# Latent attention on one core: stacked rotary scores, mask on the Vector engine, halves by shuffle, another order

## The chip, the cores and the metric

The kernel runs on one core of a Trainium2 chip. A core has a matrix engine (TensorE, "PE" in the profile, its weight loads "PEld"), a vector engine (VectorE, "DVE"), a scalar engine (ScalarE, "ACT"), GpSimd ("POOL") and a queue engine (SyncE, "SP") that here issues the transfers. The metric is the device time of one execution in microseconds; smaller is better. Before the change it was 2085.28 us, the median of three runs from 2084.88 to 2087.25.

## What is computed

A decoder of two layers over 256 positions of width 2048, all in f32. The first layer mixes positions by a gated spatial product, the second by latent attention; both attend to 256 memory tokens with 4 heads beside that, and both end in a gated feed-forward part of width 5632 with a convolution of width 3. The change lies in the second layer's attention. Cut to what matters:

```python
def apply_rope(x, cos, sin):
    x1, x2 = jnp.split(x, 2, axis=-1)
    return jnp.concatenate([x1 * cos - x2 * sin, x2 * cos + x1 * sin], axis=-1)

# key/value side, once:  kv = rmsnorm(x, g_kv) @ w_kv_a
c_kv = rmsnorm(kv[..., :512], g_kv_lat)              # latent, 512 wide
k_rope = apply_rope(kv[..., 512:], cos, sin)         # one rotary key, 64 wide, for all heads

q = (rmsnorm(q_lat, g_q_lat) @ w_uq).reshape(B, S, 12, 128 + 64)
q_rope = apply_rope(q[..., 128:], cos, sin)
qa = jnp.einsum('bqhn,rhn->bqhr', q[..., :128], w_uk)
s = (qa . c_kv + q_rope . k_rope) * 192 ** -0.5      # per head
s = jnp.where(k_pos <= q_pos, s, -inf)               # causal
p = softmax(s); o = (p . c_kv) . w_uv                # 12 heads of 128
x = x + concatenate([o, memory_attention]) @ w_out
```

## The kernel before

All activations lie transposed, features on the 128 partitions and the 256 positions along the free axis. TensorE's one-pass mode (type fp32r) keeps fewer bits than f32, so the large products split both operands into a high and a low part and sum three one-pass products: high by high, high by low, low by high (`mm_fm`, lines 137 to 143; activations hold both parts side by side, 512 wide). `chunk` loads a piece of weights (tile `raw`, 4 buffers), and ACT and DVE make its parts `whi` and `wlo`. The small products of attention are plain f32.

The second layer's mixer is `layer_b`. It runs, in this order: the latent of keys and values (`chl`), the query latent (`qhl`), the rotary key, the memory queries, a first third of the values, and then a loop over six pairs of heads. For a pair, `queries` gives two heads' 128 wide parts and, in a third block of 128 rows, both heads' rotary parts, 64 rows each. `rotary` rotates that block: a product with a permuted identity (`swap`, L744) exchanges the halves, POOL and DVE multiply with cosines and sines and add. `keys` gives the pair's keys. `scores` sums three products per block of queries in PSUM: the 128 wide part (L824), the causal mask as a bf16 product with an identity (L825), and the rotary part over 64 rows (L826); the first block of 128 queries sees 128 keys, the second 256. DVE takes the maxima (L832), ACT the exponentials with their sums (L835), DVE divides (L840). `turn` transposes the probabilities (L847) and ACT copies them out of PSUM (L849); `attend` multiplies with the values (L856 to L858) and splits the output into `mainhl`, the operand of the output projection `w_out`. `mscores`, `mturn` and `mout` do the same for the memory heads (L479, L503, L514).

The rotary key of all heads is one block of 64 columns of `w_kv_a`. `chunk(twice=True)` writes its two parts twice side by side, so that the product gives the key on both halves of the partitions, 64 rows each, and a head of either half finds it beside its own rows.

The order of work within an engine is set by a scheduler that models the program's time when it is built, starting from the order in which the code issues it. The code's own order is the loop at the end of `layer_b`: step i issues the queries and keys of pair i, the scores of pair i-1 and the turns and attends of pair i-2; the last two steps and what follows hold the four memory heads; then comes the output projection, heads 0 to 11 first and the memory heads last.

## Time and profile before

| | us |
|---|---|
| median of three runs | 2085.28 |
| the profiled execution | 2085.31 |
| its span (first to last instruction) | 2083.5 |
| TensorE busy in it | 2064.8 |
| DVE, ACT, POOL busy | 1341.7, 1063.4, 108.6 |

A line of the profile's groups names the source line, the engine, the operation, the tile written and those read, the shapes, the number of instructions, their busy time and mean length, and behind the second bar the idle time of the engine ahead of them with what ended it. A line of the timeline has the start and the length in microseconds from the span's start, then the same names; equal instructions that follow each other are merged, and an idle time stands in brackets. Records of products overlap on TensorE, so the distance between two starts, not a record's length, is what a product takes.

### The profile page before, as it was taken

How to read it: one execution, taken by the hardware profiler on the slowest of the kernel's cores; microseconds unless marked ns; L12 is line 12 of the kernel's file. 1: busy time of each engine (PE TensorE's matmuls, PEld its weight loads, DVE VectorE, ACT ScalarE, POOL GpSimd, SP SyncE). 2: the span in 40 equal slices, each digit the busy share in tenths (PEclk: the TensorE clock that was granted, in tenths of full speed). 3: DMA queues.
4: the chain of work that ended last, by engine and by line, in shares of the span. 5: the costliest groups of instructions: out<-in, count | busy, mean ns of one | idle time of the engine just before them, and what ended most of it. 6: DMA issues, size and time to landing. Idle time of an engine off the chain costs nothing.

```text
span 2083.5 us, 39410 instructions
## 1 busy us (share of the span) xinstructions
PE 2064.8 (99%) x16368; PEld 1985.9 (95%) x16368; DVE 1341.7 (64%) x1828; ACT 1063.4 (51%) x1434; POOL 108.6 (5%) x137
## 2 busy tenths in 40 slices
PE   8999999999999999999999999999999999999998
PEld 7989999999999999999999989999988999889996
DVE  6656666766646666467688655676664576655765
ACT  7654644555434554345556555455543555535554
POOL 0000012100000000000052111210000000000000
PEclk9999999999999999999999999999999999999999
DMA  8566556666656666566556534566666666666664
GB/s 275 178 205 189 162 181 197 190 199 191 198 193 192 194 193 200 189 196 193 186 189 187 173 107 133 193 192 187 188 198 196 190 195 193 194 194 193 192 189 151
DMA packets 207575, 392.54 MB, mean 188 GB/s; under 512 B 14302, under 2 KB 22820, under 8 KB 207268
## 3 DMA queue, kind: packets, MB, share of 16 engines
q1 hardware_dynamic: 207252, 389.50, 60.6%
q8 instruction: 128, 2.10, 0.4%
q14 instruction: 51, 0.42, 0.1%
q10 hardware_dynamic: 144, 0.52, 0.1%
HBM read 387.88 MB, written 2.10 MB: 187 GB/s over the span
## 4 chain that ended last, share of the span: by engine, by line
PE 98%; ACT 1%; DMA 0%; issue 0%; DVE 0%; SPq 0%; ACTq 0%
PE ps L141 26%; PE ps L140 26%; PE ps L143 26%; PE ps L171 6%; PE ps L173 6%; PE ps L172 6%; PE ps L826 1%; PE ps L824 1%; DMA raw<-in_w_mem_kv 0%; PE ps L514 0%; PE ps L479 0%; PE ps L659 0%; ACT whi L124 0%; ACT junk L396 0%; PE ps L847 0%
## 5 line engine op out<-in xcount | busy, mean ns | idle before, releaser
L120 DVE TENSOR_TENSOR wlo<-raw,whi 128x1024 fp32r<-128x1024 f32 x660 | 808.4, 1242 | 634.2 <-issue 439.3
L119 ACT ACTIVATE whi<-raw 128x1024 fp32r<-128x1024 f32 x660 | 695.3, 1060 | 785.6 <-PE ps L141 598.0
L140 PE MATMUL ps<-xhl,whi 128*128 128x256 f32 x3280 | 756.1, 277 | 0.0
L141 PE MATMUL ps<-xhl,whi 128*128 128x256 f32 x3280 | 754.3, 276 | 0.0
L141 PEld LDWEIGHTS ps<-xhl,whi 128*128 128x128 f32 x3280 | 615.8, 188 | 0.3
L140 PEld LDWEIGHTS ps<-xhl,whi 128*128 128x128 f32 x3280 | 615.6, 188 | 0.3
L143 PE MATMUL ps<-xhl,wlo 128*128 128x256 f32 x3280 | 406.7, 276 | 0.0
L143 PEld LDWEIGHTS ps<-xhl,wlo 128*128 128x128 f32 x3280 | 387.7, 188 | 0.2
L140 PE MATMUL ps<-h,whi 128*128 128x256 f32 x704 | 161.6, 276 | 0.0
L141 PE MATMUL ps<-h,whi 128*128 128x256 f32 x704 | 161.5, 276 | 0.0
L569 DVE SCALAR_TENSOR_TENSOR c<-a,cT,c 128x255 f32<-128x255 f32 (+1 forms) x352 | 146.1, 477 | 0.0
L172 PE MATMUL ps<-wlo,h 128*128 128x512 f32 x352 | 136.8, 389 | 0.0
L173 PE MATMUL ps<-whi,h 128*128 128x512 f32 x352 | 136.6, 389 | 0.0
L171 PE MATMUL ps<-whi,h 128*128 128x512 f32 x352 | 136.3, 389 | 0.0
L141 PEld LDWEIGHTS ps<-h,whi 128*128 128x128 f32 x704 | 132.0, 188 | 0.0
L140 PEld LDWEIGHTS ps<-h,whi 128*128 128x128 f32 x704 | 131.9, 188 | 0.0
L566 ACT ACTIVATE c<-a,cT 128x256 f32<-128x256 f32 x176 | 91.7, 592 | 75.8 <-DVE a L210 75.8
L140 PE MATMUL ps<-mainhl,whi 128*128 128x256 f32 x512 | 117.9, 276 | 0.0
L141 PE MATMUL ps<-mainhl,whi 128*128 128x256 f32 x512 | 117.7, 276 | 0.0
L125 DVE SCALAR_TENSOR_TENSOR wlo<-raw,gT,whi 128x512 fp32r<-128x512 f32 x112 | 84.5, 801 | 31.6 <-ACT whi L124 28.8
L124 ACT ACTIVATE whi<-raw,gT 128x512 fp32r<-128x512 f32 x112 | 74.9, 717 | 42.2 <-PE ps L141 18.3
L141 PEld LDWEIGHTS ps<-mainhl,whi 128*128 128x128 f32 x512 | 96.1, 188 | 0.0
(256 smaller groups left out, 2060.8 us busy)
## 6 DMA issues: line engine op xcount, KB each, us to landing
raw<-in_w_ffn_up SPq DMA_DIRECT2D x352, 512.0 KB, 3.9
raw<-in_w_ffn_down SPq DMA_DIRECT2D x176, 512.0 KB, 4.4
raw<-in_w_out SPq DMA_DIRECT2D x64, 512.0 KB, 4.0
raw<-in_w_in_a SPq DMA_DIRECT2D x56, 512.0 KB, 3.8
raw<-in_w_mem_kv SPq DMA_DIRECT2D x32, 512.0 KB, 5.2
raw<-in_w_in_b SPq DMA_DIRECT2D x16, 512.0 KB, 4.0
raw<-in_w_uq SPq DMA_DIRECT2D x12, 384.0 KB, 3.0
raw<-in_w_kv_a SPq DMA_DIRECT2D x8, 512.0 KB, 3.8
```

What stands on the lines that cost most here:

```text
L119: nc.scalar.activation(hi[:, :n], raw[:, :n], AF.Copy)
L120: nc.vector.tensor_tensor(lo[:, :n], raw[:, :n], hi[:, :n].bitcast(F32), ALU.subtract)
L124: nc.scalar.activation(hi[:, s], raw[:, s], AF.Copy, scale=gains[k])
L125: nc.vector.scalar_tensor_tensor(lo[:, s], raw[:, s], gains[k], hi[:, s].bitcast(F32), ALU.mult, ALU.subtract)
L140: mm(acc, wh, x[:, :S], start=first, stop=False)
L141: mm(acc, wh, x[:, S:], start=False, stop=False)
L143: mm(acc, wl, x[:, :S], start=False, stop=last)
L171: mm(acc, xh, wh, start=first, stop=False)
L172: mm(acc, xh, wl, start=False, stop=False)
L173: mm(acc, xl, wh, start=False, stop=last)
L566: nc.scalar.activation(c[:, i, :], a[:, i, :], AF.Identity, scale=w(2), bias=w(3))
L569: nc.vector.scalar_tensor_tensor(o, a[:, i, : S - 2 + j], w(j), o, ALU.mult, ALU.add)
```

## The change

The rotary key, the rotary query, the mask and the order of the loop change; all else stays.

*Scores.* A rotated query block of a head is split into its high and low parts, and the two are stacked: for the first head of a pair the high part on rows 0 to 63 and the low part on rows 64 to 127, for the second head the other way round. The key is split likewise into `krs[:, 0]`, its high part on both halves of the rows, and `krs[:, 1]`, its low part on both. Two one-pass products of 128 rows then sum all four products of parts. The mask, -1e30 above the diagonal, is an SBUF tile; one DVE instruction adds it to the scores, writes the sum to `p` and takes the maximum, followed by a read of the accumulator. The exponentials read `p` instead of PSUM.

*Halves.* The host lays out the columns of `w_kv_a` and `w_uq` so that the two halves of a rotary part lie 16 rows apart within 32; a DVE shuffle exchanges them, and DVE does the multiplying and adding. Since the columns of a pair are now in the order in which they are used, `chunk` splits a piece of `w_uq` by one instruction on ACT and one on DVE instead of two.

*Rotary key.* The 64 columns' high and low parts are stacked side by side as one block of 128 columns, each multiplied by both parts of the activations; a product with a folded identity (`fold`) then adds the halves and writes the sum to both.

*Order.* The scores, turns and memory heads of a step are issued as below; the value projections 1 and 2 move to steps 2 and 4, and the output projection starts with the memory heads and takes the last two heads in between.

```diff
         if twice:
-            ...
+            both = hi[:, : 2 * n].rearrange("p (k o c) -> p k o c", o=2, c=ncol)
             for k in range(nk):
-                ...
+                r, h = view(raw)[:, k, :], both[:, k, 0, :]
+                nc.scalar.activation(h, r, AF.Copy, scale=gains[k])
+                nc.vector.scalar_tensor_tensor(both[:, k, 1, :], r, gains[k], h.bitcast(F32), ALU.mult, ALU.subtract)
+            return hi[:, : 2 * n].rearrange("p (k c) -> p k c", k=nk)
...
-            def rotate(dst, a):
-                acc = self.psum()
-                mm(acc[:, :S], self.swap, a, start=True, stop=True)
-                m = self.tmp(lb, [P, S], "rm", 2)
-                nc.gpsimd.tensor_tensor(m, a, self.cosT, ALU.mult)
-                tt(dst, acc[:, :S], self.sinT, ALU.mult)
-                nc.gpsimd.tensor_tensor(dst, dst, m, ALU.add)
+            def rotate(a):
+                other = self.tmp(lb, [P, S], "rs", 2)
+                nc.vector.stream_shuffle(other, a, [i ^ 16 for i in range(32)])
+                r = self.tmp(lb, [P, S], "rm", 2)
+                tt(r, a, self.cosT, ALU.mult)
+                tt(other, other, self.sinT, ALU.mult)
+                tt(r, r, other, ALU.add)
+                return r
...
-                h, l = self.chunk(self.rows(wkv, KR, ROPE)(c, 8), 8, ROPE, [gk(c + i) for i in range(8)], twice=True)
-                self.mm_fm([(acc, h[:, i, :], l[:, i, :], x(c + i), c + i == 0, c + i == NB - 1) for i in range(8)])
-            tt(kr, acc, rb, ALU.mult)
+                both = self.chunk(self.rows(wkv, KR, ROPE)(c, 8), 8, ROPE, [gk(c + i) for i in range(8)], twice=True)
+                for i in range(8):
+                    for o in range(2):
+                        mm(acc, both[:, i, :], x(c + i)[:, o * S : (o + 1) * S], start=c + i + o == 0, stop=c + i + o == NB)
+
+            def rotary_key():
+                nc.scalar.activation(kr, acc, AF.Copy)
+                sums = self.psum()
+                mm(sums[:, :S], self.fold, kr, start=True, stop=True)
+                tt(kr, sums[:, :S], rb, ALU.mult)
+                r = rotate(kr)
+                nc.scalar.activation(krs[:, 0, :], r, AF.Copy)
+                tt(krs[:, 1, :], r, krs[:, 0, :].bitcast(F32), ALU.subtract)
...
+                r = rotate(accs[2])
+                qr[pr] = self.tmp(lp, [P, 2, S], "qr", 2, F32R)
+                for j in range(2):
+                    own, far = (slice(o * ROPE, (o + 1) * ROPE) for o in (j, 1 - j))
+                    nc.scalar.activation(qr[pr][own, j, :], r[own, :], AF.Copy)
+                    tt(qr[pr][far, j, :], r[own, :], qr[pr][own, j, :].bitcast(F32), ALU.subtract)
...
                     mm(o, qn[pr][:, j, q], kn[pr][:, j, :n], start=True, stop=False)
-                    mm(o[:, qb * P :], self.identb, self.maskb, start=False, stop=False)
-                    mm(o, qr[pr][rows, q], krT[rows, :n], start=False, stop=True)
+                    for i in range(2):
+                        mm(o, qr[pr][:, j, q], krs[:, i, :n], start=False, stop=i == 1)
...
-                    nc.vector.tensor_reduce(mx[:, qb : qb + 1], sc[:, part[qb]], AX.X, ALU.max)
+                    nc.vector.tensor_tensor_reduce(
+                        p[:, part[qb]], sc[:, part[qb]], self.mask[:, part[qb]], 1.0, -3e38, ALU.add, ALU.max, mx[:, qb : qb + 1]
+                    )
...
-                mm(o[:, :P], v[:, 0, cols], pT[:, :P], start=True, stop=True)
-                mm(o[:, P:S], v[:, 0, cols], pT[:, P:S], start=True, stop=False)
+                mm(o[:, :S], v[:, 0, cols], pT[:, :S], start=True, stop=False)
                 mm(o[:, P:S], v[:, 1, cols], pT[:, S : S + P], start=False, stop=True)
...
+            for i in range(n):
+                queries(i)
+                keys(i)
+                if i >= 2:
+                    turn(2 * i - 4)
+                    turn(2 * i - 3)
+                if i in (2, 4):
+                    values(i // 2)
+                if i >= 1:
+                    scores(2 * i - 2)
+                    scores(2 * i - 1)
+                if i >= 2:
+                    attend(2 * i - 4)
+                    attend(2 * i - 3)
+                if i < MH:
+                    mscores(i)
+                if 1 <= i <= MH:
+                    mturn(i - 1)
+                if 2 <= i <= MH + 1:
+                    mout(i - 2)
+            each = lambda f, *hs: [lambda h=h: f(h) for h in hs]
+            for f in each(scores, 10, 11) + each(turn, 8, 9) + each(attend, 8, 9):
+                f()
+            hooks = {0: each(turn, 10, 11), 2: each(attend, 10, 11)}
+            self.w_out(1, hl, [12, 13, 14, 15] + list(range(12)), hooks)
             ctx.close()
-            self.w_out(1, hl, list(range(NB)))
```

The new line numbers are some ten lower or higher than the old; the same code is named by both where needed. How the built programs stand, at three places. First TensorE at the scores: before, one head (`kn` keys, `qn` the 128 wide queries, `krT` the rotary key, `qr` the rotary query).

```order
L824 MATMUL ps_13944<-kn_13774,qn_13731 128x128
L825 LDWEIGHTS identb
L825 MATMUL ps_13944<-maskb,identb 128x128
L826 MATMUL ps_13944<-krT,qr_13864 128x128
L824 MATMUL ps_13944<-kn_13774,qn_13731 128x256
L825 LDWEIGHTS identb
L825 MATMUL ps_13944<-maskb,identb 128x128
L826 MATMUL ps_13944<-krT,qr_13864 128x256
```

Now the same place for two heads (L826 is now the 128 wide part, L828 the stacked rotary products).

```order
L826 MATMUL ps_14231<-kn_13967,qn_13954 128x128
L828 MATMUL ps_14231<-krs,qr_13962 128x128 x2
L826 MATMUL ps_14231<-kn_13967,qn_13954 128x256
L828 MATMUL ps_14231<-krs,qr_13962 128x256 x2
L826 MATMUL ps_14249<-kn_13967,qn_13954 128x128
L828 MATMUL ps_14249<-krs,qr_13962 128x128 x2
L826 MATMUL ps_14249<-kn_13967,qn_13954 128x256
L828 MATMUL ps_14249<-krs,qr_13962 128x256 x2
```

A head has six products as before; the two masks and the two 64-row products have become four one-pass products.

Second, TensorE at the end of the loop, before: turns (L847) and attends (L856 to L858) of heads 10 and 11 and the last memory heads.

```order
L847 MATMUL ps_14725<-ident,p_14662 128x128 x3
L479 MATMUL ps_14731<-kT_83,qm_12641 128x256 x2
L479 MATMUL ps_14744<-kT_83,qm_12641 128x256 x2
L847 MATMUL ps_14757<-ident,p_14680 128x128 x3
L856 MATMUL ps_14763<-pT_14729,scratch 128x128
L857 MATMUL ps_14763<-pT_14729,scratch 128x128
L858 MATMUL ps_14763<-pT_14729,scratch 128x128
L856 MATMUL ps_14769<-pT_14761,scratch 128x128
L857 MATMUL ps_14769<-pT_14761,scratch 128x128
L858 MATMUL ps_14769<-pT_14761,scratch 128x128
L503 MATMUL ps_14775<-ident,mp_14737 128x128 x4
L503 MATMUL ps_14782<-ident,mp_14750 128x128 x4
```

Now the end of the loop is the scores of head 11, the turns (L850) and attends (L859, L860) of heads 8 and 9, and the first products of the output projection (L130, L131).

```order
L826 MATMUL ps_14685<-kn_14571,qn_14558 128x128
L828 MATMUL ps_14685<-krs,qr_14566 128x128 x2
L826 MATMUL ps_14685<-kn_14571,qn_14558 128x256
L828 MATMUL ps_14685<-krs,qr_14566 128x256 x2
L850 MATMUL ps_14703<-ident,p_14625 128x128 x3
L850 MATMUL ps_14709<-ident,p_14643 128x128 x3
L859 MATMUL ps_14715<-pT_14707,scratch 128x256
L860 MATMUL ps_14715<-pT_14707,scratch 128x128
L859 MATMUL ps_14720<-pT_14713,scratch 128x256
L860 MATMUL ps_14720<-pT_14713,scratch 128x128
L130 MATMUL ps_14727<-mainhl_13597,whi_14730 128x256
L131 MATMUL ps_14727<-mainhl_13597,whi_14730 128x256
```

No memory head is left here, and nothing stands between the last transpose of heads 8 and 9 and their attends.

Third, ACT at the same place, now: `p_14676` and `p_14694` are the probabilities of heads 10 and 11, `pT_14707` and `pT_14713` the turned ones of heads 8 and 9.

```order
L204 ACTIVATE mainhl_13597<-ps_14652 128x256
L838 ACTIVATE p_14643,den_14642<-p_14643,mx_14641 128x128
L838 ACTIVATE p_14643,den_14642<-p_14643,mx_14641 128x256
L204 ACTIVATE mainhl_13597<-ps_14657 128x256
L204 ACTIVATE mainhl_13597<-ps_14662 128x256
L838 ACTIVATE p_14676,den_14675<-p_14676,mx_14674 128x128
L838 ACTIVATE p_14676,den_14675<-p_14676,mx_14674 128x256
L852 ACTIVATE pT_14707<-ps_14703 128x384
L852 ACTIVATE pT_14713<-ps_14709 128x384
L838 ACTIVATE p_14694,den_14693<-p_14694,mx_14692 128x128
L838 ACTIVATE p_14694,den_14693<-p_14694,mx_14692 128x256
```

The exponentials of head 10 stand ahead of the copies of the turned heads 8 and 9, and those of head 11 behind them.

124 lines of the change are left out of this document (45 added, 79 removed).

## The prediction

> **What bounds the kernel now.** I read the page first: the busy shares, then the chain of waits.
>
> ```profile
> span 2083.5 us, 39410 instructions
> PE 2064.8 (99%) x16368; PEld 1985.9 (95%) x16368; DVE 1341.7 (64%) x1828; ACT 1063.4 (51%) x1434; POOL 108.6 (5%) x137
> PE 98%; ACT 1%; DMA 0%; issue 0%; DVE 0%; SPq 0%; ACTq 0%
> ```
>
> TensorE is busy for 99% of the span and is 98% of the chain that ends last. A change of this kernel is therefore worth what it takes from, or adds to, TensorE's stream of products, plus what TensorE waits. Next the table by stretches, cut where the second layer's latent attention begins (key/value side and query latents until 1160, the loop over head pairs until 1265).
>
> ```profile
> 1083.00:1160.00 77.00, 77.00 (x656) 76.14 (x656) 67.65 (x121) 44.51 (x90) 19.78 (x18) 1.00 0.59 181
> 1160.00:1265.00 105.00, 103.39 (x705) 88.66 (x704) 64.64 (x159) 61.42 (x152) 13.25 (x12) 1.00 0.38 113
> ```
>
> Columns: length, busy us of PE, weight loads, DVE, ACT, POOL (instructions), granted clock, DMA share, GB/s. The clock is full in both. The loop is the only stretch of the two in which PE is not wholly busy, and DVE and ACT work there for 64.6 and 61.4 us of 105. Matmul records overlap, so I price products by the distance from one start to the next in the timeline, not by their duration.
>
> **What a product costs.** Timeline rows (start, length, line, tiles, shape, records). A plain f32 product takes two records, a one-pass (fp32r) product one.
>
> ```profile
> 1185.78 1.07 PE L143 MATMUL ps<-chl,wlo 128*128 128x256 f32 x8
> 1186.69 0.38 PE L824 MATMUL ps<-kn,qn 128*128 128x128 f32 x2
> ...
> 1204.49 0.39 PE L858 MATMUL ps<-pT,scratch 128*128 128x128 f32 x2
> ...
> 1204.96 0.28 PE L140 MATMUL ps<-qhl,whi 128*128 128x256 f32 x1
> ...
> 1257.28 1.89 PE L479 MATMUL ps<-kT,qm 128*128 128x256 f32 x8
> 1259.01 0.49 PE L847 MATMUL ps<-ident,p 128*128 128x128 f32 x3
> 1259.34 0.39 PE L856 MATMUL ps<-pT,scratch 128*128 128x128 f32 x2
> ```
>
> One-pass, 256 columns: (1186.69 - 1185.78) / 8 = 0.114 us. Plain f32, 256 columns: (1259.01 - 1257.28) / 8 = 0.216 a record, 0.43 a product. Transposes of 128 columns: 0.33 / 3 = 0.11. Passing between the two kinds is free within 0.02: from L858 at 1204.49 to the third one-pass record at 1204.96 are 0.47, and one f32 product of 128 columns (0.22, below) and two one-pass ones (0.23) make 0.45.
>
> **Term 1, the scores.** Two heads, then the attend that follows:
>
> ```profile
> 1212.65 0.39 PE L824 MATMUL ps<-kn,qn 128*128 128x128 f32 x2
> ...
> 1213.72 0.70 PE L824 MATMUL ps<-kn,qn 128*128 128x256 f32 x2
> 1214.25 0.22 PE L825 MATMUL ps<-maskb,identb 128*128 128x128 bf16 x1
> 1214.40 0.70 PE L826 MATMUL ps<-krT,qr 64*128 64x256 f32 x2
> 1215.03 0.23 PE L825 MATMUL ps<-maskb,identb 128*128 128x128 bf16 x1
> ...
> 1216.92 0.49 PE L856 MATMUL ps<-pT,scratch 128*128 128x128 f32 x2
> 1217.24 0.39 PE L857 MATMUL ps<-pT,scratch 128*128 128x128 f32 x2
> 1217.46 0.39 PE L858 MATMUL ps<-pT,scratch 128*128 128x128 f32 x2
> ```
>
> An f32 product of 128 columns is 1217.46 - 1217.24 = 0.22. The rotary product L826, only 64 rows high, takes 0.63 (1214.40 to 1215.03) where full height takes 0.43: it is 0.1 late at each record, and the product behind it is late too (the first L856 takes 0.32, not 0.22). So a pair of heads costs 1217.24 - 1212.65 - 0.22 = 4.37, six pairs 26.2 us. After the change a head is an f32 product of 128 columns (0.22) and one of 256 (0.43), two one-pass products of 256 columns (0.23) and two of 128. The mask product and the 64-row products are gone. A one-pass product of 128 columns is nowhere in this trace. Below: the transposes' 0.11; above: a plain f32 product of the same width, 0.22. I take 0.113, since every one-pass row is a single record and the 256-column one needs no more than that. A head is then 0.22 + 0.43 + 0.23 + 0.23 = 1.11, twelve 13.3, and 26.2 - 13.3 = **12.9 us saved**; at the upper bound 24 x 0.11 = 2.6 less.
>
> The Trainium skill speaks against this step: "TensorE: Matmul & The Clock Gate", Part 3, says that a weight load overlaps matmuls in flight only where the two use different row groups, and full-height operands all share theirs. By that rule the 48 stacked loads would stand open. The trace differs: the full-height products at 1257.28 follow each other at 0.216 with nothing exposed, and the 64-row ones are the late ones.
>
> **Term 2, the halves' exchange.** Seven exchange products leave TensorE, one fold product comes in:
>
> ```profile
> 1178.07 0.59 PE L744 MATMUL ps<-qn,swap 128*128 128x256 f32 x2
> 1178.31 0.58 PE L171 MATMUL ps<-whi,chl 128*128 128x512 f32 x1
> 1178.73 0.40 PE L172 MATMUL ps<-wlo,chl 128*128 128x512 f32 x1
> 1178.96 0.39 PE L173 MATMUL ps<-whi,chl 128*128 128x512 f32 x1
> ```
>
> The exchange and one 512-column pass take 0.66, such a pass 0.23, so the exchange 0.43. Six fewer: **2.6 us**.
>
> **Term 3, the rotary key.** 48 one-pass products become 32: 16 x 0.114 = **1.8 us**. The 16 small scalings on ACT and DVE that go with them, and the key's rotation, now behind the fold, lie beside TensorE, which never idles in that stretch (77.00 of 77.00); the rotated key is first read by the first scores (1186.69 now), long after the stretch ends at 1160. Without that cover the key's chain would cost about 3 us once.
>
> **Term 4, waits.** Three now, all at the end of the loop:
>
> ```profile
> 1253.60 1.04 PE L503 MATMUL ps<-ident,mp 128*128 128x128 f32 x8
> 1255.13 1.99 PE L514 MATMUL ps<-pT,mv 128*128 128x256 f32 x8 [0.49 <-ACT pT L507]
> ...
> 1259.79 0.39 PE L858 MATMUL ps<-pT,scratch 128*128 128x128 f32 x2
> 1260.79 0.49 PE L856 MATMUL ps<-pT,scratch 128*128 128x128 f32 x2 [0.62 <-ACT pT L849]
> ...
> 1261.57 0.60 PE L503 MATMUL ps<-ident,mp 128*128 128x128 f32 x4
> 1262.66 0.72 PE L503 MATMUL ps<-ident,mp 128*128 128x128 f32 x4 [0.49 <-DVE mp L495]
> ```
>
> Start to start less the work between: 1.53 - 0.87, 1.00 - 0.22, 1.09 - 0.44, together 2.1, some 2.4 with the first record after each wait, which is 0.1 late. In the new order the memory heads are spread over the loop, and heads 10 and 11 are turned and attended inside the output projection, whose 48 products ahead of each (5.4 us) cover their softmax. Those three waits go. What is late next is the attend of heads 8 and 9: TensorE does the scores of 10 and 11, six transposes, and then needs the evicted transposes, and ACT has the exponentials of head 10 queued ahead of that eviction.
>
> ```profile
> L849 ACT ACTIVATE pT<-ps 128x384 f32<-128x384 f32 x12 | 5.8, 485 | 1.8 <-PE ps L847 1.8
> L835 ACT ACTIVATE p<-ps,mx 128x256 f32<-128x256 f32 x12 | 5.6, 468 | 0.0
> L835 ACT ACTIVATION_READ_ACCUMULATOR p<-ps,mx 128x1 f32 x24 | 4.8, 200 | 0.0
> L832 DVE TENSOR_REDUCE mx<-ps 128x1 f32<-128x256 f32 x12 | 5.0, 413 | 0.0
> L832 DVE TENSOR_REDUCE mx<-ps 128x1 f32<-128x128 f32 x12 | 3.5, 290 | 11.9 <-PE ps L826 11.9
> L801 DVE COPY qn<-ps 128x256 f32<-128x256 f32 x6 | 2.5, 424 | 4.0 <-PE ps L143 3.3 <-issue 0.7
> L747 DVE TENSOR_TENSOR qr<-ps,sinT 128x256 f32<-128x256 f32 x6 | 2.5, 422 | 0.4 <-PE ps L744 0.3
> ```
>
> From the end of head 10's scores: the two masked maxima on DVE, 0.7 (as L832 now) to 1.1 (each with an accumulator read of 0.2, as ACT's), their scaling and the hand-overs about 0.5, two exponentials about 1.0, the eviction 0.5: 2.7 to 3.1. TensorE meanwhile has head 11's scores (1.11) and six transposes (0.66), 1.8. It waits 0.9 to 1.3, and up to 1.3 more if DVE still has the splits of three earlier outputs ahead (3 x 0.42). Behind the waiting eviction on ACT stand the second eviction and head 11's exponentials; the second attend has the first one's 0.65 as cover. I take 1.9 here and 0.5 for the first transposes of the loop, where the pipeline starts with less behind it: 2.4, so this term is **zero**, between 2 lost and 2 gained. The value projections, moved with their four weight DMAs behind two later steps, and the memory scores are the same work elsewhere; DMA is at 0.38 in the loop, and the queue gets no more bytes.
>
> **What is added beside TensorE.** Per pair DVE gets a shuffle, three products and sums and two 64-row differences in place of a copy and a product. By L801 and L747 that is four more at 0.42, 1.7 a pair, 10.1 in all. The masked maximum stands for the plain one; with the reads (2 x 0.2 a head) 4.8 more. A shuffle is not in this trace: at least 0.42 like the copy, twice that if both sides are slow. So DVE has 64.6 + 14.9 = 79.5 us in a loop of about 105 - 15.5 = 89.5: close, but not the bound. ACT gains twelve 64-row copies, some 0.4 each, 4.8 us onto 61.4. POOL loses its share. What hides all this is TensorE's own work between a pair's queries and its scores: the next pair's queries and keys alone are 60 passes of 0.114, 6.8 us.
>
> **Sum:** 12.9 + 2.6 + 1.8 + 0 = 17.3. The profiled execution took 2085.31, its span 2083.5, so 1.8 lie around it; the median of the runs is 2085.28, the same. 2083.5 - 17.3 + 1.8 = **2068.0 us**.
>
> **Rivals.**
> *Narrow one-pass products cost what f32 ones do* (0.22): 2.6 less, 2070.6. For it: no row shows them; against it: they are one record.
> *The late 0.1 stays*: if it comes from a product's neighbours and not its height, each of the 48 stacked products keeps 0.1, 4.8 us: 2072.8. Against it: the free passages above. The skill's rule quoted above leads to the same place.
> *DVE runs behind in the densest steps*: if the 30 new instructions (six shuffles, 24 masked maxima) are dearer by 0.5 each, 15 us fill the 10 us that DVE has left and put 5 on the path: 2073. For it: 79.5 of 89.5 leaves little room, and DVE takes its work in order.
> *DVE becomes the bound, slower than before*: in the loop over pairs, the same 30 instructions. The 10 us left and the 17.3 gained are eaten from 27.3 / 30 = 0.9 us each above what I took; at 1.2 above, 36 - 27.3 gives 8.7 us over before, 2094. Against it: nothing of this width on DVE takes over 0.5 in the rows above.
>
> **How the numbers follow.** Forecast 0.6; narrow products 0.18; neighbours 0.05; DVE behind 0.13; DVE the bound 0.04. The forecast alone spans 2065 to 2071; the range takes in the next three up to 2074: 2064.5 to 2074. This kernel's runs tell about 0.2% (4 us) from no change: faster 0.94, same 0.03, slower 0.03.
>
> **What would show it.** Timeline of a score pair: about 2.2 us instead of 4.37, one-pass products at 0.11 apart. No exchange products, no bf16 mask. In the list of waits one wait of one to two us for an evicted transpose behind the scores of heads 10 and 11, and none in the output projection. DVE at about 80 us in the loop. Wrong would be: narrow products at 0.22, or waits for DVE spread over the steps.

## The result and the profile after

The changed kernel takes 2067.79 us, the median of four runs from 2067.30 to 2069.34; the kernel before, in the same series, 2085.09 (four runs, 2084.88 to 2087.25). The ratio is 0.9914, with a 95% interval from 0.9902 to 0.9926. That is 17.3 us less; 2068.0 us was forecast. The profiled execution took 2069.34 us. Its page, after the change: span, busy times, and the chain that ended last by engine.

```profile
span 2067.6 us, 39221 instructions
...
PE 2048.7 (99%) x16292; PEld 1979.6 (96%) x16292; DVE 1346.7 (65%) x1868; ACT 1064.4 (51%) x1420; POOL 93.2 (5%) x122
...
PE 98%; ACT 1%; DMA 0%; SPq 0%; DVE 0%; issue 0%; DVEq 0%; ACTq 0%
```

TensorE still bounds the kernel, and it is busy 16.1 us less. The span is only 15.9 us shorter, since this one execution came 1.7 us later to the second layer (1094.77 against 1093.03 in the rows below), 1.1 of it in one wait of the first layer, far ahead of the changed code (for `memhl`: 1.3 us before, 2.4 after). This wait differs from execution to execution, also where the first layer's code is the same (1.0 to 2.6 us in the runs below that are made from the changed kernel). I therefore compare a stretch that it doesn't touch: from the first product of the second layer (the sum of squares) to the last product of all. Timeline rows, before:

```profile
1093.03 0.59 PE L244 MATMUL ps<-ssum,ones 128*128 128x256 f32 x2
...
2074.15 0.39 PE L173 MATMUL ps<-whi,h 128*128 128x512 f32 x1
```

and after:

```profile
1094.77 0.59 PE L234 MATMUL ps<-ssum,ones 128*128 128x256 f32 x2
...
2058.22 0.39 PE L163 MATMUL ps<-whi,h 128*128 128x512 f32 x1
```

981.12 us have become 963.45: 17.7 us less, and this is the number that the parts below have to make up. I divided the stretch by adding up, group by group, the distances from the start of each matmul record to the start of the next one. So a wait counts for the group in front of it, and a record that is late too. "Key side" is all from the start of the stretch to the first query product, "memory" the memory heads' three kinds of products. What follows the output projection is 722.09 us in every kernel here.

| us | key side | scores | exchange | turns, attends | memory | queries, keys, values | output projection | stretch |
|---|---|---|---|---|---|---|---|---|
| before | 68.62 | 24.99 | 2.40 | 12.84 | 10.16 | 52.87 | 87.16 | 981.12 |
| after | 66.81 | 13.38 | 0 | 12.76 | 7.84 | 53.32 | 87.25 | 963.45 |
| difference | -1.81 | -11.61 | -2.40 | -0.08 | -2.32 | +0.45 | +0.09 | -17.67 |

One thing shifts between the columns. Where an f32 product stands in front of a one-pass one, the distance behind its last record is 0.03 us instead of 0.22 (256 columns) or 0.11 (128), and the rest of its time is counted with the group behind. Timeline after:

```profile
1197.76 1.03 PE L504 MATMUL ps<-pT,mv 128*128 128x256 f32 x4
1198.44 0.47 PE L130 MATMUL ps<-qhl,whi 128*128 128x256 f32 x1
```

Four records of 0.216 make 0.86, and the distance is 0.68. The memory heads, spread over the loop, have five such places after and one before, the exchange of before has one. Counted where it belongs, the exchange is 2.6 less, memory 1.7 less, and queries, keys and values differ by 0.1.

The loop over pairs of heads, as a window of the profile after (the columns are those of the prediction's):

```profile
1160.00:1265.00 105.00, 103.79 (x784) 98.97 (x783) 74.81 (x211) 72.07 (x161) 0.00 (x0) 1.00 0.44 139
```

DVE does 74.8 us where it did 64.6, ACT 72.1 where it did 61.4, and TensorE idles for 1.2 us. (The window now ends inside the output projection, so part of this is the splitting of its weights: up to 1246.90, just ahead of that projection, DVE does 67.9.) The pair of heads that the prediction priced, in the timeline after:

```profile
1206.09 0.39 PE L826 MATMUL ps<-kn,qn 128*128 128x128 f32 x2
1206.23 0.42 PE L828 MATMUL ps<-krs,qr 128*128 128x128 f32 x2
1206.49 0.65 PE L826 MATMUL ps<-kn,qn 128*128 128x256 f32 x2
1206.78 0.59 PE L828 MATMUL ps<-krs,qr 128*128 128x256 f32 x2
...
1208.32 0.60 PE L859 MATMUL ps<-pT,scratch 128*128 128x256 f32 x2
1208.75 0.38 PE L860 MATMUL ps<-pT,scratch 128*128 128x128 f32 x2
```

From 1206.09 to 1208.32 are 2.23 us, where 2.2 were forecast and 4.37 stood before. Taking off the f32 products (2 x 0.65) and the 256-column one-pass products (4 x 0.114) leaves 0.47 for four narrow ones, 0.12 each. The attend behind isn't late (1208.32 to 1208.75: 0.43).

One wait is left in the loop, the forecast one. TensorE and ACT at the end of the loop, in the timelines after:

```profile
1243.72 0.82 PE L850 MATMUL ps<-ident,p 128*128 128x128 f32 x6
1245.74 0.70 PE L859 MATMUL ps<-pT,scratch 128*128 128x256 f32 x2 [1.21 <-ACT pT L852]
1246.28 0.38 PE L860 MATMUL ps<-pT,scratch 128*128 128x128 f32 x2
```

```profile
1244.33 0.40 ACT L838 ACTIVATE p<-p,mx 128x128 f32<-128x128 f32 x1 [1.76 <-DVE mx L836]
...
1245.22 0.85 ACT L852 ACTIVATE pT<-ps 128x384 f32<-128x384 f32 x2
```

The six transposes need 0.66, so they end about 1244.4; ACT has begun the exponentials of head 10 just before and copies the transposes out only behind them. TensorE loses 2.02 - 0.66 = 1.4, and 0.1 more in the late first record behind (0.54 instead of 0.43).

### The profile page after: what moved, and what is told of

It is laid out like the page before. It is cut to its first block, busy times and chain, and to the rows that moved or that the text cites. A ratio compares the mean times of both kernels' runs of the same rounds, so it can differ in the third digit from the quotient of the medians.

```text
span 2067.6 us, 39221 instructions
## 1 busy us (share of the span) xinstructions
PE 2048.7 (99%) x16292; PEld 1979.6 (96%) x16292; DVE 1346.7 (65%) x1868; ACT 1064.4 (51%) x1420; POOL 93.2 (5%) x122
## 4 chain that ended last, share of the span: by engine, by line
PE 98%; ACT 1%; DMA 0%; SPq 0%; DVE 0%; issue 0%; DVEq 0%; ACTq 0%
PE ps L131 26%; PE ps L130 26%; PE ps L133 26%; PE ps L161 6%; PE ps L163 6%; PE ps L162 6%; DMA raw<-in_w_mem_kv 0%; PE ps L826 0%; PE ps L504 0%; PE ps L469 0%; PE ps L859 0%; PE ps L649 0%; PE ps L828 0%; ACT whi L114 0%; PE ps L850 0%; ACT junk L386 0%
## 5 line engine op out<-in xcount | busy, mean ns | idle before, releaser
L110 DVE TENSOR_TENSOR wlo<-raw,whi 128x1024 fp32r<-128x1024 f32 (+1 forms) x672 | 818.7, 1235 | 631.8 <-issue 433.5
L109 ACT ACTIVATE whi<-raw 128x1024 fp32r<-128x1024 f32 (+1 forms) x672 | 705.4, 1056 | 788.6 <-PE ps L131 589.3
L130 PE MATMUL ps<-xhl,whi 128*128 128x256 f32 x3264 | 752.3, 277 | 0.0
L131 PE MATMUL ps<-xhl,whi 128*128 128x256 f32 x3264 | 750.6, 276 | 0.0
L130 PEld LDWEIGHTS ps<-xhl,whi 128*128 128x128 f32 x3264 | 612.7, 188 | 0.3
L131 PEld LDWEIGHTS ps<-xhl,whi 128*128 128x128 f32 x3264 | 612.7, 188 | 0.3
L130 PE MATMUL ps<-h,whi 128*128 128x256 f32 x704 | 161.6, 276 | 0.0
L131 PE MATMUL ps<-h,whi 128*128 128x256 f32 x704 | 161.5, 276 | 0.0
L130 PEld LDWEIGHTS ps<-h,whi 128*128 128x128 f32 x704 | 132.0, 188 | 0.0
L131 PEld LDWEIGHTS ps<-h,whi 128*128 128x128 f32 x704 | 131.9, 188 | 0.0
L130 PE MATMUL ps<-mainhl,whi 128*128 128x256 f32 x512 | 118.0, 277 | 0.0
L131 PE MATMUL ps<-mainhl,whi 128*128 128x256 f32 x512 | 117.7, 276 | 0.0
L130 PEld LDWEIGHTS ps<-mainhl,whi 128*128 128x128 f32 x512 | 96.1, 188 | 0.0
```

The source lines that it names most:

```text
L109: nc.scalar.activation(hi[:, :n], raw[:, :n], AF.Copy)
L110: nc.vector.tensor_tensor(lo[:, :n], raw[:, :n], hi[:, :n].bitcast(F32), ALU.subtract)
L130: mm(acc, wh, x[:, :S], start=first, stop=False)
L131: mm(acc, wh, x[:, S:], start=False, stop=False)
```

## Experiments

Each kernel is one edit away from the kernel before, or from the changed one ("after"), and is timed beside runs of the kernel before on the same chip (medians 2085.4 to 2085.7). What a single wait or product is worth is read in the stretch defined above.

| us | median (lowest to highest) | ratio to before, 95% | stretch | scores | exchange | turns, attends | memory | queries, keys, values |
|---|---|---|---|---|---|---|---|---|
| e1, from before | 2079.71 (2078.88 to 2081.36) | 0.9958 to 0.9982 | 975.17 | 17.93 | 2.80 | 12.52 | 10.63 | 53.43 |
| e2, from before | 2082.82 (2081.62 to 2083.78) | 0.9976 to 0.9994 | 977.67 | 21.39 | 2.39 | 13.10 | 10.04 | 52.88 |
| e8, from after | 2078.76 (2077.50 to 2079.12) | 0.9948 to 0.9977 | 973.35 | 23.70 | 0 | 12.42 | 7.94 | 53.15 |
| e10, from e6 | 2070.56 (2068.64 to 2071.12) | 0.9908 to 0.9941 | 965.05 | 15.93 | 0 | 11.70 | 7.94 | 53.23 |
| e4, from after | 2076.85 (2076.71 to 2078.66) | 0.9945 to 0.9973 | 972.68 | 13.38 | 2.09 | 12.39 | 7.83 | 60.40 |
| e4b, from after | 2071.95 (2070.57 to 2073.06) | 0.9918 to 0.9948 | 966.88 | 13.38 | 2.69 | 12.85 | 7.84 | 53.57 |
| e5, from after | 2069.44 (2068.53 to 2070.58) | 0.9907 to 0.9934 | 964.79 | 13.38 | 0 | 12.85 | 7.83 | 52.92 |
| e3, from after | 2072.99 (2071.06 to 2073.44) | 0.9919 to 0.9946 | 967.63 | 13.37 | 0 | 13.88 | 10.66 | 53.67 |
| e9, from before | 2082.38 (2081.43 to 2083.51) | 0.9975 to 0.9992 | 977.54 | 22.86 | 2.58 | 12.69 | 7.90 | 53.55 |
| e6, from after | 2066.33 (2066.10 to 2068.09) | 0.9893 to 0.9920 | 962.31 | 13.38 | 0 | 11.27 | 7.84 | 53.33 |
| e7, three more | 2067.85 (2066.96 to 2069.36) | 0.9901 to 0.9930 | 963.16 | 13.39 | 0 | 12.74 | 7.83 | 53.05 |
| e7, eight more | 2069.73 (2068.84 to 2070.77) | 0.9908 to 0.9941 | 964.71 | 14.61 | 0 | 12.58 | 8.34 | 53.02 |

### Is a 64-row product late because of its height (e1)?

The kernel before, with the rotary query of each head laid in a tile of 128 rows whose other half is zero. The products are otherwise those of before.

```diff
+            qz = [lp.tile([P, 2, S], F32, name=f"qz{i}") for i in range(2)]
+            for z in qz:
+                nc.gpsimd.memset(z, 0.0)
...
-                rotate(qr[pr], qn[pr][:, 2, :])
+                rotate(r, qn[pr][:, 2, :])
+                qr[pr] = qz[pr % 2]
+                for j in range(2):
+                    own = slice(j * ROPE, (j + 1) * ROPE)
+                    nc.gpsimd.tensor_copy(qr[pr][own, j, :], r[own, :])
...
-                    mm(o, qr[pr][rows, q], krT[rows, :n], start=False, stop=True)
+                    mm(o, qr[pr][:, j, q], krT[:, :n], start=False, stop=True)
```

> The kernel before, with one thing changed: the rotary product is 128 rows high instead of 64 (each head's rotary query lies in a tile whose other 64 rows are zero; POOL copies it there). Product kinds, mask and order stay. Theory (the 64-row height makes its records and the product behind it late by 0.1 us): the 24 rotary products fall from 0.63 and 0.42 us to 0.43 and 0.22, 4.8 us, and the 24 products behind them by 0.1, 2.4 us; about 7 us less, 2078. Rival (the lateness comes from the neighbours of another kind): no change, 2085.

Measured: 2079.71 us. The scores fall by 7.06, about what the first theory said. Timeline of the end of a head's scores and the first two products behind:

```profile
1213.85 0.22 PE L831 MATMUL ps<-maskb,identb 128*128 128x128 bf16 x1
1213.90 0.65 PE L832 MATMUL ps<-krT,qz 128*128 128x256 f32 x2
1214.39 0.38 PE L862 MATMUL ps<-pT,scratch 128*128 128x128 f32 x2
1214.61 0.39 PE L863 MATMUL ps<-pT,scratch 128*128 128x128 f32 x2
```

Mask and rotary product take 0.54 together, where the same two took 0.78 before (1214.25 to 1215.03), and the product behind takes 0.22 instead of 0.32. The products beside it and the arithmetic are the same, only the height is new: the lateness goes with the height. This run takes away the 64-row records and the changes between 64 and 128 rows together, so it does not tell which of the two is late; e8 below does. The stretch shortens by less, 5.95. A part of the 1.1 between them is 0.5 more in the memory heads: TensorE comes to them earlier and waits, at L514 for its evicted transposes 1.0 us, where it was 0.49. (The exchange takes 0.4 more and queries, keys and values 0.6 more, turns and attends 0.3 less; why is not shown.) The longer wait is the first sign that the old order would not have kept all of the gain.

### Mask on DVE alone (e2)

The kernel before, with the masked maximum and the exponentials of the change, and without the bf16 products.

```diff
-                    mm(o[:, qb * P :], self.identb, self.maskb, start=False, stop=False)
...
-                    nc.vector.tensor_reduce(mx[:, qb : qb + 1], sc[:, part[qb]], AX.X, ALU.max)
+                    nc.vector.tensor_tensor_reduce(
+                        p[:, part[qb]], sc[:, part[qb]], self.mask[:, part[qb]], 1.0, -3e38, ALU.add, ALU.max, mx[:, qb : qb + 1]
+                    )
```

> The kernel before, with the mask added on DVE in the masked maximum and the 24 bf16 mask products gone; the 64-row f32 rotary products stay. Theory: 24 mask products at 0.15 us from start to start, 3.6 us less: 2081.5. Rival (the products pay what the mask product hid, or the longer softmax shows at the end of the loop): 2083 to 2085.

Measured: 2082.82 us by the medians, 2.6 below before. In the stretch it is 3.45, and 3.60 in the scores. That is the theory's number, but not its reason. e2's timeline, the first pair of heads from its start to the product behind it, and a place in a later pair:

```profile
1186.52 0.38 PE L821 MATMUL ps<-kn,qn 128*128 128x128 f32 x2
...
1190.59 0.38 PE L140 MATMUL ps<-qhl,whi 128*128 128x256 f32 x1
...
1213.05 0.70 PE L822 MATMUL ps<-krT,qr 64*128 64x256 f32 x4
```

The first pair takes 4.07 us. Before, the same pair took 4.29 (from 1186.69, a row of the prediction):

```profile
1190.98 0.39 PE L140 MATMUL ps<-qhl,whi 128*128 128x256 f32 x1
```

So four mask products are worth 0.22, 0.05 each and 1.3 us in all, though the distance from the start of one to the next start was 0.15. The other five pairs of e2 take 3.46 each. Without the masks in between, 64-row products of two heads came to lie next to each other there and ran together (four records from 1213.05 to 1213.68). In the kernel before this happens in one pair, which takes 3.64 (shown under e8 and e10). The remaining 2.3 us of the 3.60 come from that, and not from the mask. DVE's longer instruction shows in no wait of TensorE: its waits at the end of the loop are 1.5 us together, where they were 1.6.

### Stacked or apart (e8), and side by side (e10)

Three products of 64 rows, high by high, high by low and low by high, in place of two stacked ones, in the changed kernel:

```diff
-                    own, far = (slice(o * ROPE, (o + 1) * ROPE) for o in (j, 1 - j))
-                    nc.scalar.activation(qr[pr][own, j, :], r[own, :], AF.Copy)
-                    tt(qr[pr][far, j, :], r[own, :], qr[pr][own, j, :].bitcast(F32), ALU.subtract)
+                    own = slice(j * ROPE, (j + 1) * ROPE)
+                    nc.scalar.activation(qr[pr][own, 0, :], r[own, :], AF.Copy)
+                    tt(qr[pr][own, 1, :], r[own, :], qr[pr][own, 0, :].bitcast(F32), ALU.subtract)
...
-                    for i in range(2):
-                        mm(o, qr[pr][:, j, q], krs[:, i, :n], start=False, stop=i == 1)
+                    for i, k in ((0, 0), (0, 1), (1, 0)):
+                        mm(o, qr[pr][own, i, q], krs[own, k, :n], start=False, stop=i == 1)
```

> The kernel after, with the two stacked products of a block of queries replaced by three one-pass products of 64 rows (high by high, high by low, low by high; the low by low product is left out). Theory (height): each 64-row record is 0.1 us late and so is the product behind the three: per block 3 x 0.21 + 0.1 in place of 0.23, 0.5 us, times 24 = 12 us more: 2080. Rival (height does not matter for one-pass products): one more pass per block, 24 x 0.11 = 2.7 us: 2070.5.

Measured: 2078.76 us, the scores at 23.70. A pair of heads in e8's timeline:

```profile
1209.16 0.39 PE L826 MATMUL ps<-kn,qn 128*128 128x128 f32 x2
...
1210.58 0.61 PE L829 MATMUL ps<-krs,qr 64*128 64x256 f32 x3
1211.13 0.49 PE L826 MATMUL ps<-kn,qn 128*128 128x128 f32 x2
...
1213.21 0.70 PE L860 MATMUL ps<-pT,scratch 128*128 128x256 f32 x2
```

4.05 us instead of 2.23. Its twelve 64-row records cost (4.05 - 1.30) / 12 = 0.23 each on the average, the stacked ones 0.93 / 8 = 0.12. But the three at 1210.58 are not late alike. The last two of them, and the last one alone, as narrower windows of the timeline show them:

```profile
1210.81 0.39 PE L829 MATMUL ps<-krs,qr 64*128 64x256 f32 x2
1210.92 0.27 PE L829 MATMUL ps<-krs,qr 64*128 64x256 f32 x1
```

The distances from 1210.58 are 0.23, 0.11 and 0.21 (to 1211.13). The one in the middle is that of a full-height product, and so it is in every group of three in e8. The lateness lies where 64 and 128 rows meet, not at every 64-row record. A passage to 64 rows and back costs 0.34 here, (4.05 - 1.30 - 12 x 0.116) / 4, with three records in it. In the prediction's pair of before (1212.65 to 1216.92) it costs 0.31 with two, (4.27 - 2 x 1.30 - 4 x 0.11) / 4, where 2 x 1.30 are all its f32 products at their full-height price and 0.11 is a mask's price between full-height products (e1: 0.54 - 0.43). The prediction's 0.1 a record and 0.1 behind gives the same 0.3 for two records, and 0.4 for three; for twelve heads the theory's 12 us came out as 10.3 in the scores (13.38 to 23.70).

Without the stacking, the one-pass mode and the mask on DVE would have gained 1.3 of the 11.6 us (24.99 to 23.70), no more than the mask alone in e2.

In one place of the kernel before, 64-row products of two heads ran in each other's time. Its timeline there:

```profile
1250.04 0.70 PE L826 MATMUL ps<-krT,qr 64*128 64x256 f32 x4
```

Four records, two heads' products, take 0.63 (to 1250.67), what two take elsewhere. The two heads of a pair lie on different row halves. e10 makes this the rule, on top of e6 below:

```diff
+                if h % 2:
+                    return
+                sc = [self.psum(), self.psum()]
...
+                    for j in range(2):
+                        mm(sc[j][:, part[qb]], qn[pr][:, j, q], kn[pr][:, j, :n], start=True, stop=False)
+                    for i, k in ((0, 0), (0, 1), (1, 0)):
+                        for j in range(2):
+                            own = slice(j * ROPE, (j + 1) * ROPE)
+                            mm(sc[j][:, part[qb]], qr[pr][own, i, q], krs[own, k, :n], start=False, stop=i == 1)
```

> The kernel with the late turns (e6, 2066.33 us) with the rotary products of a pair of heads taken apart again: three one-pass products of 64 rows a head and block (high by high, high by low, low by high; the product of the two low parts is left out), those of the two heads, which lie on different row halves, issued alternately. Theory: products on different row halves run side by side, as two records of before in one place did. A pair of heads then has six slots of two products, each slot between 0.11 and 0.21 us, beside its 1.3 us of f32 products: 1.96 to 2.56 us where the stacked products make 2.23. Six pairs: 1.6 less to 2.0 more, 2064.7 to 2068.3 us. Rival: a 64-row record is 0.1 us late whatever runs beside it, so twelve records at 0.21 make 2.5 and a pair 3.8 us: 9.5 us more, 2076 us.

Measured: 2070.56 us, 4.2 above e6 by the medians and 2.7 in the stretch. Neither theory's time holds, but the mechanism of the first does. e10's timeline:

```profile
1206.77 0.61 PE L827 MATMUL ps<-kn,qn 128*128 128x128 f32 x4
1207.31 0.55 PE L831 MATMUL ps<-krs,qr 64*128 64x128 f32 x6
1207.79 1.13 PE L827 MATMUL ps<-kn,qn 128*128 128x256 f32 x4
1208.85 0.62 PE L831 MATMUL ps<-krs,qr 64*128 64x256 f32 x6
1209.40 0.70 PE L866 MATMUL ps<-pT,scratch 128*128 128x256 f32 x2
```

Six records take 0.55 (1208.85 to 1209.40), as three did in e8 (1210.58 to 1211.13): two at a time. The Trainium skill, "TensorE: Matmul & The Clock Gate", section "Why this matters for your kernels", says that products of few rows on distinct row groups run at the same time; the trace agrees. But a pair of heads takes 2.63, against 2.23 stacked. Each change of height still costs: the four f32 records ahead of the 64-row ones take 0.54 (1206.77 to 1207.31), and those between them 1.06 (1207.79 to 1208.85), where 0.44 and 0.87 are their price, and the slots of the 64-row ones 1.03 where six of 0.116 would be 0.70. That is 0.3 for each of the two passages, as in e8. Filling the rows with the low parts is cheaper than running the halves side by side.

### What the shuffle saves (e4, e4b)

The changed kernel, with the halves exchanged by a product again. The columns are in the new layout, so the permuted identity is another one; DVE copies the rotary block out of PSUM for it.

```diff
-                nc.vector.stream_shuffle(other, a, [i ^ 16 for i in range(32)])
-                tt(r, a, self.cosT, ALU.mult)
-                tt(other, other, self.sinT, ALU.mult)
+                b = self.tmp(lb, [P, S], "ra", 2)
+                nc.vector.tensor_copy(b, a)
+                turned = self.psum()
+                mm(turned[:, :S], self.swap, b, start=True, stop=True)
+                tt(r, b, self.cosT, ALU.mult)
+                tt(other, turned[:, :S], self.sinT, ALU.mult)
```

> The kernel after, with the halves exchanged by a product with a permuted identity on TensorE (after a copy out of PSUM) instead of the shuffle on DVE; the fold stays. Theory: seven more f32 products of 256 columns at 0.43 us, 3.0 us: 2070.8. Rival (the product waits for DVE's copy and the rotated query comes late): 2073 or more, with waits for DVE in TensorE's list.

Measured: 2076.85 us, the rival's side: three times the price of the products. e4's list of waits and one of its timeline rows:

```profile
PE ps L744 <- DVE ra L742: 4.4, 6, 1.8
```

```profile
1176.03 0.70 PE L744 MATMUL ps<-ra,swap 128*128 128x256 f32 x2 [1.78 <-DVE ra L742]
```

The exchange stands right behind the queries, so TensorE waits for a copy that DVE makes in its own order, six times, and the waits appear in the column of the queries: 60.40, 7.1 more, of which 4.4 are these waits and 1.1 is time of the exchange products themselves, shifted as said above. Whether that is the place or the work was open. e4b leaves the work and issues the exchange behind the same step's keys:

```diff
-                r = rotate(accs[2])
+                qr[pr] = held(accs[2])
+
+            def rotary(pr):
+                r = rotate(qr[pr])
...
                 keys(i)
+                rotary(i)
```

> The changed kernel (2067.8 us) with the halves exchanged by a product on TensorE, as in e4 (2076.85 us), but issued behind the same step's keys, 24 one-pass products or some 2.7 us later, so that DVE's copy of the rotary part is there when TensorE comes to it. Theory: e4's excess over seven products of 0.43 us, about 6 us, was TensorE's wait for that copy and what came late behind it; here only the products are left, 7 x 0.43 = 3.0: 2070.8 us, and no wait for the copy or the products behind it. Rival: the exchange costs TensorE what e4 shows wherever it stands, since the copy and the two products that read PSUM load DVE: 2075 to 2077 us.

Measured: 2071.95 us, the stretch 3.43 above after's, where seven products of 0.43 make 3.0. From e4b's list of waits and timeline:

```profile
PE ps L747 <- DVE ra L740: 0.5, 1, 0.5
```

```profile
1205.79 0.59 PE L747 MATMUL ps<-ra,swap 128*128 128x256 f32 x2
1206.22 0.82 PE L865 MATMUL ps<-ident,p 128*128 128x128 f32 x6
```

An exchange is 0.43 there, and one wait of 0.5 is left. So 5.8 of e4's 9.2 us were its place. The shuffle itself is worth the products, and it is worth more only against an exchange that nothing covers.

### The rotary key (e5)

The changed kernel with the key's parts side by side twice, as before, and so without the fold product. (Its diff is the reverse of the part of the change on `twice` and `rotary_key`.)

> The kernel after, with the rotary key's block as before (three one-pass products of parts written twice, no fold product); the rotation by shuffle and the split of the key stay. Theory: 16 more one-pass products, 1.8 us, less the fold product of 0.43: 1.4 us more, 2069.2. Rival (the added ACT and DVE work of 16 small scalings each is not hidden): 2071 or more.

Measured: 2069.44 us, and in the stretch 1.34 above after, all of it on the key side: 16 one-pass products more, one fold product less, 1.8 - 0.43 = 1.4.

### What the order is worth (e3, e9), and its last wait (e6)

e3 is the changed kernel with the old order of the loop and of the output projection; e9 the kernel before with the new order. Their diffs are the part of the change called order, backwards and forwards; e3 keeps the new exchange and the new scores, e9 the old ones, with `rotary` of a pair issued ahead of the turns.

> The kernel after, with the loop and the output projection issued in the order of before. Theory (the waits about cancel): the three waits at the end of the loop come back, 2.1 to 2.4 us, and the one of 1.3 us ahead of the attend of heads 8 and 9 goes: about 1 us more, 2068.8. Rival (the new order is needed to hide the work that moved to DVE): 3 us or more, 2071 and up, with several waits for DVE or ACT.

> The kernel before, with the new order of the loop and of the output projection only (scores, mask, exchange and key stay). Theory (the waits about cancel): three waits of 2.1 to 2.4 us go, one of 1 to 2 us comes: about 1 us less, 2084. Rival (the order is worth more): 2082.5 or less.

Measured: e3 2072.99 us, e9 2082.38. In the stretch the old order costs 4.2 us with the new products, and the new order gains 3.6 with the old ones; both times came out on the rivals' side. e3's waits, from its list:

```profile
PE ps L850 <- DVE p L843: 1.4, 1, 1.4
PE ps L504 <- ACT pT L497: 1.0, 1, 1.0
PE ps L859 <- ACT pT L852: 0.6, 1, 0.6
PE ps L493 <- DVE mp L485: 0.5, 1, 0.5
```

These are 3.5 us; the kernel before had 1.6 of this kind in the rows that the prediction quotes. The second, 1.0, is as long in e1, where the scores are shorter and DVE has no work that it did not have before: TensorE reaches this place earlier. The first, 1.4, is new. It is the turn of head 8 (1235.25), which waits for DVE to divide the probabilities. DVE in e3's timeline:

```profile
1231.42 0.86 DVE L808 TENSOR_TENSOR qr<-rm,qr 64x256 fp32r<-64x256 f32 x2
1232.29 0.29 DVE L833 CUSTOM_DVE_ANT_0 p<-ps,mask 128x128 f32<-128x128 f32 x1
```

The scores of head 8 end at 1231.22, but DVE first makes the differences of the next rotary query, which the change gave to it, and begins the maxima 1.07 late. So most of this wait comes from the work that the change put on DVE, as the rival had it; the rest may be the shorter scores. The waits that the new order avoids are larger than the ones that were there to be read before the change. In e9 the parts are others: 1.6 us in the memory heads (2.26 in the column, with the shift), whose waits go, and 2.13 in the scores, by a thing that no theory had. The new order happened to put two heads' 64-row products side by side in five places (before: one), and they ran together as in e10: in e9's timeline four records take 0.63 (1216.64 to 1217.27).

e6 moves the turns and attends of heads 8 and 9 into the output projection too:

```diff
-            for f in each(scores, 10, 11) + each(turn, 8, 9) + each(attend, 8, 9):
+            for f in each(scores, 10, 11):
                 f()
-            hooks = {0: each(turn, 10, 11), 2: each(attend, 10, 11)}
+            hooks = {0: each(turn, 8, 9), 2: each(attend, 8, 9) + each(turn, 10, 11), 4: each(attend, 10, 11)}
```

> The kernel after, with the turns and attends of heads 8 and 9 also moved into the output projection: turns of 8 and 9 behind its first 48 products, their attends and the turns of 10 and 11 behind the next 48, the attends of 10 and 11 behind the third 48. Theory (the wait for ACT is the last one of the loop and nothing takes its place): 1.3 us less than after, 2066.5. Rival (the last chunk of the output projection waits for heads 10 and 11, or the weight splits wait for ACT): no gain, 2067.8 or more, with a wait of about 1 us for mainhl.

Measured: 2066.33 us, the fastest of all; the stretch is 1.14 below after's. Its window:

```profile
1160.00:1265.00 105.00, 105.00 (x802) 100.75 (x801) 75.18 (x208) 71.20 (x159) 0.00 (x0) 1.00 0.44 136
```

TensorE is busy for all of it. The intervals of e6 and after against before overlap, so the medians alone do not prove the 1.5 us between them. The wait that is gone is shown, 1.4 + 0.1 by the rows and 1.49 in the column of turns and attends. The stretch keeps 1.14 of it, since the output projection takes 0.3 more; e5, with the order of after, shows the same 0.3 there, so this may be a difference between executions.

### How much room DVE has (e7)

The changed kernel with three, and with eight, further masked maxima of 128x256 for each of heads 0 to 7, whose results nobody reads.

```diff
+                for _ in range(8 if h < 8 else 0):
+                    nc.vector.tensor_tensor_reduce(
+                        idle, sc[:, part[1]], self.mask[:, part[1]], 1.0, -3e38, ALU.add, ALU.max, spare
+                    )
```

> The kernel after, with three more masked maxima of 256 columns for each of heads 0 to 7 (their results are not used): 24 x 0.42 = 10 us more on DVE in the loop. Theory (DVE has room: in the steps from 1179 to 1237 of the kernel after it is busy 44 of 58 us): hidden, 2068, at most 1 us more. Rival (DVE already sets the pace in the dense steps): 4 to 8 us more, with waits for DVE spread over the steps.

> The kernel after, with eight more masked maxima of 256 columns for each of heads 0 to 7 (their results are not used): 64 x 0.42 = 27 us more on DVE in the loop, where some 14.6 us are free. Theory (DVE becomes the bound once its room is used up): about 12 us more, 2080, with waits for DVE in every step. Rival (still hidden): 2068 to 2070.

Measured: 2067.85 us with 24 more, nothing; 2069.73 with 64 more, 1.9 by the medians and 1.3 in the stretch, where 12 were expected. The same four steps as windows, after and then with 64 more:

```profile
1178.70:1237.20 58.50, 58.50 (x424) 55.14 (x423) 43.89 (x133) 41.01 (x97) 0.00 (x0) 1.00 0.42 129
```

```profile
1177.50:1236.00 58.50, 58.26 (x422) 54.65 (x421) 57.16 (x226) 40.85 (x97) 0.00 (x0) 1.00 0.41 124
```

DVE goes from 43.89 to 57.16 of 58.50 and TensorE idles for 0.24. In this window lie 48 of the added maxima with their reads, while two weight splits of 1.22 and a sum of 0.42 have moved out of it (226 - 133 = 93 = 96 - 3 instructions). So the maxima fill 13.3 + 2.9 us, 0.34 each, though one is 0.42 long and its read 0.08. DVE's timeline in after shows why:

```profile
1243.61 0.42 DVE L833 CUSTOM_DVE_ANT_0 p<-ps,mask 128x256 f32<-128x256 f32 x1
1243.95 0.08 DVE L833 DVE_READ_ACCUMULATOR2_ANT mx<- 128x1 f32 x1
```

The read starts 0.34 after the maximum, inside its 0.42. Instructions of DVE that wait for nothing overlap, as the Trainium skill, "VectorE: DVE Perf Modes", section "Two Vector instructions with no wait between them", has it for instructions that are not held. So a sum of lengths overstates how full DVE is, the more so the fuller it is: in the two windows the lengths add up to 50.9 and 73.4 us, where DVE is busy for 43.9 and 57.2. At 98% it begins to show on TensorE, by little.

## Why the prediction was right

The time, the sign and the one remaining wait came out as forecast. By its own terms, from the table of the stretch and the runs:

| | forecast | measured | by |
|---|---|---|---|
| term 1, scores | 12.9 | 12.2 | 11.61, and 0.6 of products behind that are no longer late |
| term 2, exchange | 2.6 | 2.6 | exchange column 2.40, and 0.19 of the shift (e4b: seven products and a 0.5 wait, 3.4) |
| term 3, rotary key | 1.8 | 1.8 | key side; e5 |
| term 4, waits | 0 (2 lost to 2 gained) | 1.1 | the rest of 17.7 |
| sum | 17.3 | 17.7 | medians 17.3 |

That the sum is this close is partly luck: term 1 was 0.7 too high and term 4 was 1.1 too low.

**Term 1.** After the change the scores take 13.38; 13.3 was forecast, with narrow products at 0.12 for 0.113. The rival at 0.22 is out. The rival on neighbours, with its 4.8 us, is out by the passage above without lateness, and by e1, which changes nothing but the height. What was incomplete is the reason given for the old price, 0.1 at each 64-row record: e8 shows the lateness at the changes between 64 and 128 rows, so a neighbour does matter, but one of another height. With two records to a passage the sum is the same 0.3, and the stacked products have no change of height. The mask's share was smaller than its distance of 0.15 suggests (e2: 0.05 beside 64-row products). What was too high is the side of before: 26.2 supposed six equal pairs, and in one of them, at 1250.04, two 64-row products ran together, and it took 3.64 where the others take 4.26 to 4.29. I had priced a pair from one place and not looked at the other five. The rule of the Trainium skill on open weight loads, which the prediction weighed against its rows, does not hold for full-height products here: after's 48 stacked ones take 0.12 each. The same Part 3 also names a background weight buffer, into which a load may go ahead; the prediction left that out, and no run here shows whether it is the reason.

**Terms 2 and 3** hold. For term 2, e4 shows what the sum leaves out: a product between a copy and the next work is cheap only where something covers the copy.

**Term 4** is the one that was mis-sized. The three waits of before are gone, and the attend of heads 8 and 9 waits for evicted transposes behind head 10's exponentials, as foretold. But that wait was taken as 1.9 and is 1.4 with 0.1 behind it, and the 0.5 at the first transposes did not come. The accumulator reads had been taken as ACT's 0.2 and are 0.084, and the masked maxima cost what the plain ones did (420 and 289 ns; 413 and 290 before). From after's groups:

```profile
L833 DVE CUSTOM_DVE_ANT_0 p<-ps,mask 128x256 f32<-128x256 f32 x12 | 5.0, 420 | 0.0
L833 DVE CUSTOM_DVE_ANT_0 p<-ps,mask 128x128 f32<-128x128 f32 x12 | 3.5, 289 | 3.3 <-PE ps L828 3.2
...
L833 DVE DVE_READ_ACCUMULATOR2_ANT mx<- 128x1 f32 x24 | 2.0, 84 | 0.0
```

Zero as a balance was near; zero as the worth of the order was not. I compared the waits of before with those of after, but the new products and the moved work in the old order would have waited 3.5 us (e3). The order is worth 4.2 beside the new products, and the stretch would have gained 13.5 without it.

**DVE.** 79.5 us were forecast for a loop of 89.5; DVE does 67.9 in the 86.9 up to the output projection, so it had 19 us left and not 10. That figure was wrong, and the forecast did not suffer from it, since the error was on the safe side. The two rivals in which DVE falls behind needed it to have 10 us left; e7 shows room for more than 24 further instructions of 0.5, and a loss of 1 to 2 us at 64. Their thresholds were sums of lengths, which overlap.

The column of queries, keys and values is 0.45 higher in after than before. All but 0.1 of it is the shift of f32 records described with the table; e7 with three more and e5, whose loops are alike, lie 0.3 and 0.4 below after, so the 0.1 is within what one execution differs from another.

## What to carry to other kernels

A product that uses half the rows is not half the work for TensorE: here each passage from 128 to 64 rows and back cost 0.3 us on top, and stacking the correction terms of a split product into the empty rows cost less than either leaving the rows empty or running two half products side by side. Price an edit that shortens the bounding engine together with the order around it: a shorter stream of products, or work moved onto another engine, brings the next wait closer, so the waits in the old profile can be less than what the old order will cost (1.6 us before, 2.3 in e1, 3.5 in e3). Check what an edit changes beside its own product: e2's 3.6 us looked like 24 mask products and was mostly two heads' products coming to lie side by side. Don't call an engine full by its summed lengths; load it with idle work and see where the bound begins.

## What the runs showed of the hardware that I had not expected

Two 64-row products on different halves of the rows run at the same time: six records in 0.55 us where three alone take 0.55 (e10, e8). The scheduler's order decides by chance whether a kernel with such products gets this (once in before, five times each in e2 and e9), so the price of a 64-row product read from one place need not hold at the next. A passage from 128 to 64 rows and back costs about 0.3 us, with two records in it (before), three (e8) or three pairs (e10), and a 64-row record between two others of its kind is not late (e8: 0.11). And a vector instruction of 0.42 us in a dense stretch takes 0.34, with its accumulator read of 0.08 inside that (e7).
